# Dropping tokens over capacity: the load of the positions goes behind the first copy of its queue

## The chip, the cores and the metric

The kernel runs on one core of a Trainium2 chip. The metric is the device time of one execution in microseconds (us). The core has compute engines with instruction queues of their own: PE (TensorE, matmuls), DVE (VectorE), ACT (ScalarE), POOL (GpSimd) and SP (SyncE). Transfers are done by 16 DMA engines, which all queues share. In this kernel SP and ACT issue transfers; a transfer that ACT issues stands in ACT's DMA queue (q10 in the profile), one that SP issues in SP's (q1). Each transfer is cut into rows, which are spread over the 16 engines, and each engine adds 1 to a semaphore when its part is done; so a transfer has landed when its semaphore has risen by 16.

## What is computed

```python
def reference(x, token_positions, capacity):       # x: 16 x 1024 x 512 float32
    mask = token_positions < capacity              # token_positions: 16 x 1024, capacity 256
    return (x * mask[..., np.newaxis]).astype(np.float32)
```

Each of the 16,384 tokens has a row of 512 values. A row is kept when the token's position is below the capacity, and set to zero otherwise. The positions of this input are drawn from 0 to 255, so all tokens are kept and the output equals x. The kernel may not assume this; it has to look at the positions.

## The kernel before, in words

The 16,384 rows are seen as 128 groups ("partitions") of 128 tokens (`n_per_p` is 128), so one partition holds 128 x 512 values, 256 KB in a stretch.

The kernel bets on nothing being dropped. It copies x to the output inside the DRAM, without passing through the core's memory: eight transfers of 16 tokens per partition each (L77 to L83, `C = 16`), 4 MB apiece, made of 128 rows of 32 KB. Even transfers are issued by SP, odd ones by ACT, four each. All of them count up the semaphore `s_copy`.

Beside that it finds out whether the bet holds. L72 loads the positions (64-bit integers on the device, so 256 32-bit words per partition, 128 rows of 1 KB) into the tile `tp`; this transfer is issued by ACT and has a semaphore of its own, `s_tp`. DVE waits for it (L102) and works out for every token if it is kept, in four operations over 128x128 elements: `ge`, `lt`, `low`, `keep` (L103 to L117). L119 adds the kept tokens per partition, PE adds the partitions with a matmul against ones (L123), and DVE compares the total with the number of tokens (L125): `drop_i` is 1 if any token is dropped.

SP, ACT and DVE wait for that and read `drop_i` into a register (L130 to L139). If it is 1, they load x piece by piece, multiply each token by its mask and store it over the copy (L140 to L161). If it is 0, as here, they jump over this part. Then ACT and DVE report to SP, SP reports to POOL, which clears the semaphores (L165 to L173), and SP waits for the eight copies (L174), which ends the kernel.

What sets the order around the change: no planner is at work. Each engine's instructions run in the order of the program, and the transfers of one queue stand in it in the order of their issue. The nine early transfers are collected in the list `early` and moved to the head of the program's first block (L86 to L95), ahead of the start-up of the engines, in the order of the list. So ACT's order is: the load, then copies 1, 3, 5, 7; SP's order is: copies 0, 2, 4, 6.

Of the kernel before, what the change touches and what calls it, by code (L numbers as in the profile page):

```python
# [1 line left out]

# [4 lines left out]


@with_exitstack
def kernel(  # L10
    ctx: ExitStack,
    tc: tile.TileContext,
    x: bass.AP,
    token_positions: bass.AP,
    capacity: bass.AP,
    out: bass.AP,
):
    nc = tc.nc
    P = nc.NUM_PARTITIONS
    fp32 = mybir.dt.float32  # L20
    i32 = mybir.dt.int32
    Alu = mybir.AluOpType

    x_f = x.flatten_outer_dims()
    out_f = out.flatten_outer_dims()
    N, D = x_f.shape
    n_per_p = N // P
    cap = float(int(capacity))
    x_r = x_f.rearrange("(p n) d -> p n d", p=P)
    out_r = out_f.rearrange("(p n) d -> p n d", p=P)  # L30
    tp_i32 = token_positions.rearrange("b s -> (b s)").bitcast(i32)

    sp = nc.sync
    act = nc.scalar
    ve = nc.vector
    pe = nc.tensor
    gp = nc.gpsimd


    tc.close()  # L40
    tc.compile()  # L41

    def sbuf(name, shape, dtype):
        return ctx.enter_context(nc.sbuf_tensor(name, shape, dtype)).ap()

    tp = sbuf("tp", [P, 2 * n_per_p], i32)
    ge = sbuf("ge", [P, n_per_p], fp32)
    lt = sbuf("lt", [P, n_per_p], fp32)
    low = sbuf("low", [P, n_per_p], fp32)
    keep = sbuf("keep", [P, n_per_p], fp32)  # L50
    kept = sbuf("kept", [P, 1], fp32)
    ones = sbuf("ones", [P, 1], fp32)
    drop_i = sbuf("drop_i", [1, 1], i32)
    total = ctx.enter_context(nc.psum_tensor("total", [1, 1], fp32)).ap()
    F = 16
    NBUF = 2
    n_fix = n_per_p // F
    xts = [sbuf(f"xt{b}", [P, F, D], fp32) for b in range(NBUF)]

    s_copy = nc.alloc_semaphore("s_copy")  # L60
    s_tp = nc.alloc_semaphore("s_tp")
    s_ve = nc.alloc_semaphore("s_ve")
    s_pe = nc.alloc_semaphore("s_pe")
    s_ld = [nc.alloc_semaphore(f"s_ld{b}") for b in range(NBUF)]
    s_mul = nc.alloc_semaphore("s_mul")
    s_st = [nc.alloc_semaphore(f"s_st{b}") for b in range(NBUF)]
    s_done = nc.alloc_semaphore("s_done")

    n_copy = 0
    early = []  # L70

    load_tp = act.dma_start(out=tp, in_=tp_i32.rearrange("(p w) -> p w", p=P))  # L72
    early.append(load_tp.then_inc(s_tp, 16).ins)

    C = 16  # L77
    for k in range(n_per_p // C):
        ins = (sp, act)[k % 2].dma_start(
            out=out_r[:, k * C : (k + 1) * C, :], in_=x_r[:, k * C : (k + 1) * C, :]  # L80
        ).then_inc(s_copy, 16)
        early.append(ins.ins)
        n_copy += 1  # L83


    home = nc.cur_bb.bb  # L86
    first_bb = nc.cur_f.blocks[0]
    first_sp = next(
        k for k, i in enumerate(first_bb.instructions) if i.engine == mybir.EngineType.SP
    )  # L90
    names = [i.name for i in early]
    home.instructions = [i for i in home.instructions if i.name not in names]
    first_bb.instructions = (
        first_bb.instructions[:first_sp] + early + first_bb.instructions[first_sp:]
    )  # L95

    lo = tp[:, 0 : 2 * n_per_p : 2]
    hi = tp[:, 1 : 2 * n_per_p : 2]


    ve.memset(ones, 1.0).then_inc(s_ve, 1)  # L101
    ve.wait_ge(s_tp, 16)  # L102
    ve.tensor_scalar(  # L103
        out=ge, in0=lo, scalar1=0.0, scalar2=None, op0=Alu.is_ge
    ).then_inc(s_ve, 1)
    ve.wait_ge(s_ve, 2)
    ve.scalar_tensor_tensor(  # L107
        out=lt, in0=lo, scalar=cap, in1=ge, op0=Alu.is_lt, op1=Alu.mult
    ).then_inc(s_ve, 1)
    ve.wait_ge(s_ve, 3)  # L110
    ve.scalar_tensor_tensor(  # L111
        out=low, in0=hi, scalar=0.0, in1=lt, op0=Alu.is_equal, op1=Alu.mult
    ).then_inc(s_ve, 1)
    ve.wait_ge(s_ve, 4)
    ve.scalar_tensor_tensor(  # L115
        out=keep, in0=hi, scalar=0.0, in1=low, op0=Alu.is_lt, op1=Alu.add
    ).then_inc(s_ve, 1)  # L117
    ve.wait_ge(s_ve, 5)
    ve.tensor_reduce(  # L119
        out=kept, in_=keep, axis=mybir.AxisListType.X, op=Alu.add  # L120
    ).then_inc(s_ve, 1)
    pe.wait_ge(s_ve, 6)
    pe.matmul(out=total, lhsT=ones, rhs=kept, start=True, stop=True).then_inc(s_pe, 1)  # L123
    ve.wait_ge(s_pe, 1)
    ve.tensor_scalar(  # L125
        out=drop_i, in0=total, scalar1=float(N) - 0.5, scalar2=None, op0=Alu.is_lt
    ).then_inc(s_ve, 1)


    for e in (sp, act, ve):  # L130
        e.wait_ge(s_ve, 7)
    ET = mybir.EngineType
    drop = nc.values_load(
        drop_i[0:1, 0:1],
        engines=[ET.SP, ET.Activation, ET.DVE],
        min_val=0,
        max_val=1,
        skip_runtime_bounds_check_because="a comparison gives 0 or 1",
    )  # L139
    with nc.If(drop):  # L140
        for u in range(n_fix):
            b = u % NBUF
            if u >= NBUF:
                sp.wait_ge(s_st[b], 16 * (u // NBUF))
            sp.dma_start(out=xts[b], in_=x_r[:, u * F : (u + 1) * F, :]).then_inc(s_ld[b], 16)
            ve.wait_ge(s_ld[b], 16 * (u // NBUF + 1))
            for j in range(F):
                c = u * F + j
                ve.tensor_scalar(
                    out=xts[b][:, j, :],  # L150
                    in0=xts[b][:, j, :],
                    scalar1=keep[:, c : c + 1],
                    scalar2=None,
                    op0=Alu.mult,
                ).then_inc(s_mul, 1)
            if u == 0:
                act.wait_ge(s_copy, 16 * n_copy)
            act.wait_ge(s_mul, (u + 1) * F)
            act.dma_start(out=out_r[:, u * F : (u + 1) * F, :], in_=xts[b]).then_inc(s_st[b], 16)
        for b in range(NBUF):  # L160
            act.wait_ge(s_st[b], 16 * (n_fix // NBUF))  # L161

    for e in (act, ve):  # L165
        e.sem_inc(s_done, 1)
    sp.wait_ge(s_done, 2)
    sp.sem_inc(s_done, 1)
    own = [s_tp, s_ve, s_pe, *s_ld, s_mul, *s_st, s_done]
    ids = sorted(s.num for s in own)  # L170
    assert ids == list(range(ids[0], ids[-1] + 1))
    gp.wait_ge(s_done, 3)
    gp.sem_clear(range(ids[0], ids[-1] + 1))  # L173
    sp.wait_ge(s_copy, 16 * n_copy)  # L174
    sp.sem_inc(s_copy, -16 * n_copy)


# [1 line left out]
_INS = ['x', 'token_positions', 'capacity']  # L179
_OUTS = [((16, 1024, 512), 'float32')]  # L180

_NUMBERS = {'capacity': 256}


# [26 lines left out]
```

## Time and profile before

| | |
|---|---|
| median of 5 runs | 104.58 us (104.35 to 104.81) |
| the profiled execution's own time | 104.48 us |
| its span, first to last instruction | 103.1 us |
| DMA moved in the span | 33.69 MB, mean 327 GB/s |
| HBM read and written together | 652 GB/s over the span |
| busy time of DVE, PE, POOL | 1.5, 0.2, 0.2 us |
| issue to landing of the load of the positions | 2.0 us |
| issue to landing of a copy, SP's and ACT's (median of four) | 61.4 and 67.2 us |

How to read it: the engines' busy times count the arithmetic alone; waiting and issuing transfers are not in them. A row of a DMA queue gives packets, megabytes, and the time that the queue's packets took as a share of what 16 engines have in the span (or in the window asked for). A line of waits names the waiting instruction, what it waited for, the time in total, the number of times, and the longest. "SPq" and "ACTq" are the instruction queues of SP and ACT themselves. A line of the timeline begins with the start and the duration in us.

### The profile page before, as it was taken

What the parts mean: (1) busy time and instruction counts of PE and PEld (TensorE: products, weight loads), DVE (VectorE), ACT (ScalarE), POOL (GpSimd) and SP (SyncE); (2) the same over time, 40 slices, a digit from 0 to 9 for tenths busy, and PEclk for the clock granted to TensorE, in tenths of its full rate; (3) what the DMA queues carried; (4) which work ended last, traced back from release to release, by engine and by line L of the source; (5) the groups of instructions that cost most, each with busy time, mean ns of one, the idle gap of its engine ahead of it and who ended that gap; (6) DMA issues with size and microseconds to landing.
All of it is one profiled execution on the core that took longest, in us unless ns stands there. A gap on an engine that the chain in (4) does not pass through costs nothing. (4 is left out here: it accounts for less than half of the span.)

```text
span 103.1 us, 70 instructions
## 1 busy us (share of the span) xinstructions
PE 0.2 (0%) x2; PEld 0.1 (0%) x2; DVE 1.5 (1%) x7; POOL 0.2 (0%) x4
## 2 busy tenths in 40 slices
PE   0000000000000000000000000000000000000000
PEld 0000000000000000000000000000000000000000
DVE  0230000000000000000000000000000000000000
POOL 0000000000000000000000000000000000000000
DMA  8997989989979999799699797998997998989975
GB/s 254 407 369 241 394 270 356 369 280 356 369 254 407 292 318 407 254 356 381 241 394 381 229 407 254 356 381 280 343 381 254 394 305 305 394 292 330 369 267 178
DMA packets 1297, 33.69 MB, mean 327 GB/s; under 512 B 144, under 2 KB 272, under 8 KB 272
## 3 DMA queue, kind: packets, MB, share of 16 engines
q10 hardware_dynamic: 720, 16.91, 49.7%
q1 hardware_dynamic: 576, 16.78, 48.5%
q14 instruction: 1, 0.01, 0.0%
HBM read 33.69 MB, written 33.55 MB: 652 GB/s over the span
## 5 line engine op out<-in xcount | busy, mean ns | idle before, releaser
L115 DVE SCALAR_TENSOR_TENSOR keep<-tp,low 128x128 f32<-128x128 int32 x1 | 0.3, 293 | 0.0
L107 DVE SCALAR_TENSOR_TENSOR lt<-tp,ge 128x128 f32<-128x128 int32 x1 | 0.3, 291 | 0.0
L111 DVE SCALAR_TENSOR_TENSOR low<-tp,lt 128x128 f32<-128x128 int32 x1 | 0.3, 291 | 0.0
L119 DVE TENSOR_REDUCE kept<-keep 128x1 f32<-128x128 f32 x1 | 0.3, 286 | 0.0
L103 DVE TENSOR_SCALAR ge<-tp 128x128 f32<-128x128 int32 x1 | 0.2, 227 | 0.0
L123 PE MATMUL total<-kept,ones 128*1 128x1 f32 x2 | 0.2, 164 | 6.1 <-DVE kept L119 6.1
L125 DVE TENSOR_SCALAR drop_i<-total 1x1 int32<-1x1 f32 x1 | 0.1, 147 | 0.3 <-PE total L123 0.3
L101 DVE MEMSET ones<- 128x1 f32 x1 | 0.1, 59 | 4.5 <-PEq L41 4.5
L192 POOL MEMSET const-bfloat16-1.0<- 128x1 bf16 x1 | 0.1, 101 | 0.0
L192 POOL MEMSET const-uint8-127<- 128x1 uint8 x1 | 0.1, 101 | 0.0
L192 POOL MEMSET const-float32-1.0<- 128x1 f32 x1 | 0.1, 99 | 0.0
L192 POOL MEMSET const-float32-0.0<- 128x1 f32 x1 | 0.1, 98 | 0.2 <-issue 0.2
L123 PEld LDWEIGHTS total<-kept,ones 128*1 128x1 f32 x2 | 0.1, 82 | 6.1 <-DVE kept L119 6.1
## 6 DMA issues: line engine op xcount, KB each, us to landing
out_dram<-in_x_dram SPq DMA_DIRECT2D x4, 4096.0 KB, 61.4
out_dram<-in_x_dram ACTq DMA_DIRECT2D x4, 4096.0 KB, 67.2
tp<-in_token_positions_dram ACTq DMA_DIRECT2D x1, 128.0 KB, 2.0
```

What stands on the lines that cost most here:

```text
L101: ve.memset(ones, 1.0).then_inc(s_ve, 1)
L103: ve.tensor_scalar(out=ge, in0=lo, scalar1=0.0, scalar2=None, op0=Alu.is_ge).then_inc(s_ve, 1)
L107: ve.scalar_tensor_tensor(out=lt, in0=lo, scalar=cap, in1=ge, op0=Alu.is_lt, op1=Alu.mult).then_inc(s_ve, 1)
L111: ve.scalar_tensor_tensor(out=low, in0=hi, scalar=0.0, in1=lt, op0=Alu.is_equal, op1=Alu.mult).then_inc(s_ve, 1)
L115: ve.scalar_tensor_tensor(out=keep, in0=hi, scalar=0.0, in1=low, op0=Alu.is_lt, op1=Alu.add).then_inc(s_ve, 1)
L119: ve.tensor_reduce(out=kept, in_=keep, axis=mybir.AxisListType.X, op=Alu.add).then_inc(s_ve, 1)
L123: pe.matmul(out=total, lhsT=ones, rhs=kept, start=True, stop=True).then_inc(s_pe, 1)
L125: ve.tensor_scalar(out=drop_i, in0=total, scalar1=float(N) - 0.5, scalar2=None, op0=Alu.is_lt).then_inc(s_ve, 1)
L192: nc = _bacc.Bacc("TRN2", target_bir_lowering=False, num_devices=1)
```

## The change

The load of the positions is issued by ACT after its first copy (copy 1) in place of before it. ACT's order becomes: copy 1, the load, copies 3, 5, 7. SP's order and all else stay as they are.

```diff
-    load_tp = act.dma_start(out=tp, in_=tp_i32.rearrange("(p w) -> p w", p=P))
-    early.append(load_tp.then_inc(s_tp, 16).ins)
-
     C = 16
     for k in range(n_per_p // C):
         ins = (sp, act)[k % 2].dma_start(
             out=out_r[:, k * C : (k + 1) * C, :], in_=x_r[:, k * C : (k + 1) * C, :]
         ).then_inc(s_copy, 16)
         early.append(ins.ins)
         n_copy += 1
+        if k == 1:
+            load_tp = act.dma_start(out=tp, in_=tp_i32.rearrange("(p w) -> p w", p=P))
+            early.append(load_tp.then_inc(s_tp, 16).ins)
```

## The prediction

> **What bounds the kernel now.** I read the page's head and its DMA rows first, then SP's waits, then the timeline of the first microseconds, and last the DMA view cut into short windows.
>
> ```profile
> span 103.1 us, 70 instructions
> DMA  8997989989979999799699797998997998989975
> q10 hardware_dynamic: 720, 16.91, 49.7%
> q1 hardware_dynamic: 576, 16.78, 48.5%
> ...
> SPq L175 <- SPq L175: 95.4, 1, 95.4
> SPq L133 <- DVE drop_i L125: 2.1, 1, 2.1
> ...
> 0.00 2.75 SPq L79 DMA_DIRECT2D out_dram<-in_x_dram  x4
> 0.13 0.39 ACTq L72 DMA_DIRECT2D tp<-in_token_positions_dram  x1
> 0.55 2.59 ACTq L79 DMA_DIRECT2D out_dram<-in_x_dram  x4
> 4.54 0.23 DVE L103 TENSOR_SCALAR ge<-tp 128x128 f32<-128x128 int32 x1
> 6.35 0.15 DVE L125 TENSOR_SCALAR drop_i<-total 1x1 int32<-1x1 f32 x1 [0.28 <-PE total L123]
> ```
>
> The 16 DMA engines are busy from end to end, half for q1 (SP's queue, four copies) and half for q10 (ACT's, four copies and the load: 144 packets more). SP stands at its last wait, for the copies (L175), for 95.4 of 103.1 us, so from 7.7 us on. Everything the load feeds, from ge at 4.54 to SP's arrival at 7.7, is over in 3.2 us and has 95 us to spare. The copies set the end. The load can move the time only through the DMA engines: when their stream begins, how dense it is, and how it ends. For that, the DMA view of 1.0 to 2.2 us, then of 2.2 to 5.7, then of 98.5 to 103.1, with the GB/s of four stretches between:
>
> ```profile
> q1 hardware_dynamic: 16, 0.52, 139.1%
> q10 hardware_dynamic: 144, 0.13, 34.3%
> ...
> q1 hardware_dynamic: 32, 1.05, 80.3%
> ...
> q10 hardware_dynamic: 48, 1.05, 69.2%
> q1 hardware_dynamic: 16, 0.00, 0.2%
> ...
> 1.16:1.52 0.36, 0.00 (x0) 0.00 (x0) 0.00 (x0) 0.00 (x0) 1.00 0.90 287
> 1.52:5.84 4.32, 0.00 (x0) 0.00 (x0) 1.17 (x6) 0.00 (x0) 1.00 1.08 378
> 5.84:99.70 93.86, 0.19 (x2) 0.09 (x2) 0.37 (x2) 0.00 (x0) 1.00 1.01 335
> 99.68:102.78 3.10, 0.00 (x0) 0.00 (x0) 0.00 (x0) 0.00 (x0) 1.00 0.56 180
> ```
>
> (The last two columns of the stretches are the busy share of the DMA engines and GB/s; a packet counts where it starts.) From 1.16 to 1.52 us the engines carry the load alone: 144 packets, 128 of 1 KB and 16 marks of the semaphore, 34.3% of 1.2 us, so 0.41 us on each engine. SP's first 32 KB packets begin at 1.52, as the load's go out. Until 5.84 SP's queue runs alone, three packets on each engine (48 in all); then both queues take turns, one packet each; after 99.68 only ACT's last packets are left, and the last mark falls at 102.78. From 1.16 to 102.78 is 101.6 us of nearly unbroken work.
>
> **The change part by part.** The sum is made against the profiled execution: 104.48 us, its span of 103.1 and 1.4 around it. The median of the five runs is 104.58, so 0.1 is added at the end.
>
> *ACT's issues.* The same five, in another order. Its first copy is issued at 0.13 in place of 0.55 and the load after it, at about 0.13 + 0.58 = 0.71 (ACT's four copies take 2.59 / 4 = 0.65 us each to issue, the shortest 0.58). The later three copies are issued when they are now, since the two durations are only swapped. SP's and POOL's instructions move past nothing. Cost on the path: 0.
>
> *The wait for the load.* On ACT's queue its 144 packets now stand behind the first copy's 144. That copy is issued at 0.55 and, by the DMA view of the microsecond of its issue, lands 30.2 us later, at 30.8. The load then lands at some 32 us if it goes as one turn of its queue, and at about 30.8 + 9 x 1.57 = 45 us if each of its eight rows and its mark on an engine takes a turn against a 32 KB packet of SP's (1.57 us each: 64 on an engine in 101.6 - 0.41 us, with their marks). DVE waits for it at its first real operation; behind that stand its five mask operations and the reduction, PE's matmul, drop_i, then the branch on SP, ACT and DVE, POOL's clearing, and SP's wait for the copies. None of them issues a DMA when nothing is dropped, which is this case: 16.78 MB per queue is all the copying there is. The 3.2 us after landing end at 48 us at the latest. One instruction load of 8 KB is in the trace at 13.8 us, 6 us after the branch; were it to follow the branch, it would come at 54. The cover is the copies until 102.8, so 48 us are left and this costs 0. If the cover were gone, the price would be 3.2 us beyond the load's landing.
>
> *The front of the stream.* Taken out: 0.41 us of small packets ahead of the copies. The question is when SP's first packet can start without them. No row shows it. Lower bound 1.16, where the first packet of any kind starts now; upper bound 1.52, where SP's does now. Nearest row: the load's issue ends at 0.13 + 0.39 = 0.52 and its packets begin 0.64 later; SP's first issue ends at about 0.62 (the median of its four), and 0.62 + 0.64 = 1.26. I take 1.26: the stream begins 0.10 later than now, bounds 0 and +0.36.
>
> *The small packets in the middle.* The same 0.41 us on each engine now lie among large packets. If they cost what they cost now, the length of 101.6 stays as it is: 0. Low bound -0.41: they vanish in the shadow of the other queue's packets, which is not excluded, since a 32 KB packet runs at 32.8 KB / 1.57 us = 20.9 GB/s an engine on the average but SP's alone, in the stretch from 3.22 to 4.45 us, at 453 / 16 = 28: the engines wait on something shared and could catch up. High bound +0.41: each costs double under load. The 112 marks of the copies that fall among large packets show no cost that I can find, which is why I stay at 0.
>
> *The end of the stream.* If the load takes nine turns, SP's queue gains nine packets on ACT's, and ACT's runs alone for about nine more packets at the end, some 14 us in place of the present 3. Is one queue alone slower? Alone at the front: 378 GB/s against 335 with both, so 1.39 us for a round of 16 packets against 1.565: 9 x -0.18 = -1.6 us. Alone at the end: 1.05 MB from about 98.9 to 102.4, 300 GB/s, 1.75 a round: 9 x +0.18 = +1.6. The front has the ramp in it and the end the stragglers, both close to neither; I take 0 and keep half of each, -0.8 and +0.8.
>
> The row on turns is the alternation of single 32 KB packets after 5.84 us. The Trainium skill ("DMA: Bandwidth & Descriptors", Queues, rings and completion order) says that an engine goes round its queues packet by packet, and that a packet is typically some 9 to 17 descriptors. By that, the load's eight rows and mark on an engine could be one turn; the end of the stream would then stay as it is and its term would be 0 for certain, where by the alternation of single descriptors it is the widest term of the sum. Here every 32 KB row is a turn of its own, so for rows of 32 KB this trace does not show such packets; for rows of 1 KB it leaves the question open.
>
> Sum: 0 + 0 + 0.10 + 0 + 0 = +0.1; 104.48 + 0.1 + 0.1 for the median = 104.7 us. Bounds added in full: -1.2 to +1.6.
>
> **The rivals.** A measurement of this kernel (104.35 to 104.81) tells about 0.3%, 0.31 us, from no change; so the marks are 104.27 and 104.89.
> - *Forecast: hidden.* 104.7, own range 104.3 to 104.9. For it: the bytes are the same, and the load has 48 us to spare.
> - *Slower at the front.* SP's first packet is not ready before 1.5 us whatever ACT does; the 0.41 us ahead of it were free, and are now paid among the copies: +0.36, 104.9 to 105.1. For it: SP issues first, at 0.00, and yet its packets come after the load's. Against: they start just as the load's run out, as if held by them. It decides from a start of about 1.4 us on.
> - *Slower at the end.* ACT's queue trails by nine packets and runs alone at the 300 GB/s of the last microseconds: +0.8, 105.5. It decides if a round alone costs 0.035 us more than a shared one (9 x 0.035 = 0.31). For it: the last two rounds. Against: the first three.
> - *Faster.* The small packets vanish among the large ones while the copies begin at 1.26, 0.3 us sooner than now: -0.3; with a lone queue as quick as at the front, -0.8 more is possible: 104.2 to 103.6.
> - *The load decides the end.* It would have to land after 99 us; only one copy of four stands before it. 105 to 107, next to excluded.
>
> **How the numbers follow.** Forecast 0.39. Slower at the front 0.19, at the end 0.18, the load at the end 0.01: together 0.38. Faster 0.23. The range leaves out the far half of "faster" and the far half of "slower at the end": 104.0 to 105.5.
>
> **What the changed profile would show.** ge on DVE starting after 30 us (near 32: one turn; near 45: nine), and SP's last wait shorter by as much: the wait's step right. First DMA packets at 1.26 and of 32 KB: the front right; at 1.5: the first rival. q1's last mark before 90 us with q10 alone behind it: nine turns; then the GB/s of that stretch against 335 decides between the third rival and the fourth. A span of 103.2 with all this is the forecast. It is wrong if the rate with both queues itself changes with the lag between them, which no row of before can show: 1% of it is 1 us.

## The result: 104.74 us, 0.21% over before

The changed kernel takes 104.74 us in the median (104.30 to 105.50, 52 runs), the kernel before, over all its runs beside it, 104.54 us. The ratio is 1.0021, with a 95% interval from 1.0013 to 1.0030: slower by 0.14 to 0.31 us. That lies within the 0.3% that the forecast counts as no change, with a real cost of 0.22 us inside it. A later set of runs on another chip gave 1.0026 (1.0008 to 1.0044). The levels differ from chip to chip (before takes 105.5 to 105.7 us on the chips of the experiments), so below only ratios to before on the same chip are compared, and one profile stands for one execution: the profiled one of the change took 104.95 us, 0.47 us more than the profiled one of before (104.48). That is twice the measured difference, so a cost of 0.2 us is read from the ratios; the traces show only where time could go.

The profile after, in the order of the reading before: the page's DMA rows, SP's and DVE's waits, the timeline.

```profile
span 103.6 us, 70 instructions
q1 hardware_dynamic: 576, 16.78, 48.7%
q10 hardware_dynamic: 720, 16.91, 48.4%
...
SPq L176 <- SPq L176: 58.2, 1, 58.2
SPq L134 <- DVE drop_i L126: 39.4, 1, 39.4
DVE ge L104 <- DMA tp<-in_token_positions_dram: 37.3, 1, 37.3
...
0.12 0.61 ACTq L75 DMA_DIRECT2D out_dram<-in_x_dram  x1
0.77 0.74 ACTq L82 DMA_DIRECT2D tp<-in_token_positions_dram  x1
1.54 1.99 ACTq L75 DMA_DIRECT2D out_dram<-in_x_dram  x3
42.24 0.23 DVE L104 TENSOR_SCALAR ge<-tp 128x128 f32<-128x128 int32 x1 [37.26 <-DMA tp<-in_token_positions_dram]
```

The bytes and packets are the same. The wait for the load is there, 37.3 us of DVE, and ge starts at 42.24 in place of 4.54. SP reaches its last wait 37 us later and still stands there for 58.2 us. So the wait costs nothing. The page's own chain names it nonetheless ("DMA tp", 40% of the span): its last piece is drop_i, before the change as after it, and the copies that set the end are not in it.

What the DMA engines did is seen in the stretches (the last two columns are their busy share and GB/s), and in the DMA view of 29.0 to 40.5 us, where the load is carried:

```profile
1.16:1.38 0.22, 0.00 (x0) 0.00 (x0) 0.00 (x0) 0.00 (x0) 1.00 0.00 0
1.38:4.41 3.03, 0.00 (x0) 0.00 (x0) 0.00 (x0) 0.00 (x0) 1.00 0.99 346
5.84:29.20 23.36, 0.00 (x0) 0.00 (x0) 0.00 (x0) 0.00 (x0) 1.00 1.01 334
42.26:87.88 45.62, 0.19 (x2) 0.09 (x2) 1.52 (x6) 0.00 (x0) 1.00 1.00 333
89.30:101.80 12.50, 0.00 (x0) 0.00 (x0) 0.00 (x0) 0.00 (x0) 1.00 1.00 336
...
q1 hardware_dynamic: 128, 3.67, 94.6%
q10 hardware_dynamic: 128, 0.13, 4.0%
```

The stream begins at 1.38 us; from 1.16, where it began before with the load, to there the engines are idle. In the lower view q1's 128 packets are 7 rounds of copies (a round is one packet on each of the 16 engines) and 16 marks, and q10's 128 are the eight rows of the load on each engine: one turn each, with a packet of SP's between each two, and once SP's mark. The load's packets take 4.0% of 11.5 us, 0.46 us an engine. (In a second trace of the changed kernel, on another chip, they take 3.3% of the 11.0 us from 30.7 to 41.7, 0.36 us.) SP's queue thus gains about eight packets, its last mark falls at 88.54, and from 89.3 to 101.8 ACT's queue runs alone: at 336 GB/s, against 333 with both (328 and 331 in the second trace).

### The profile page after: what moved, and what is told of

Its sections match the earlier page's. It is cut to its first block, busy times and chain, and to the rows that moved or that the text cites. A ratio compares the mean times of both kernels' runs of the same rounds, so it can differ in the third digit from the quotient of the medians.

```text
span 103.6 us, 70 instructions
## 1 busy us (share of the span) xinstructions
PE 0.2 (0%) x2; PEld 0.1 (0%) x2; DVE 1.6 (2%) x7; POOL 0.2 (0%) x4
## 5 line engine op out<-in xcount | busy, mean ns | idle before, releaser
L104 DVE TENSOR_SCALAR ge<-tp 128x128 f32<-128x128 int32 x1 | 0.2, 228 | 37.3 <-DMA tp<-in_token_positions_dram 37.3
```

Source lines behind the costliest of these rows:

```text
L104: ve.tensor_scalar(out=ge, in0=lo, scalar1=0.0, scalar2=None, op0=Alu.is_ge).then_inc(s_ve, 1)
```

## The experiments

Three accounts of the 0.2 us stood against each other. **Front / bytes:** the load's 0.131 MB cost their time at the stream's rate (0.39 us at 333 GB/s) wherever they lie among copies, but ahead of the copies they lie in time in which the engines would be idle for the most part (the first expectations call it "front", the later ones "bytes"). **End:** the queue that trails and runs alone is dearer. **Dear:** small packets among large ones cost more than their bytes.

**No load.** `load_tp` is left out and DVE fills the tile with zeros:

```diff
-    load_tp = act.dma_start(out=tp, ...)
+    ve.memset(tp, 0).then_inc(s_tp, 16)
```

> The load of the positions is left out: DVE fills the tile with zeros and counts as before, so the positions are not looked at. It gives the whole price of the load, ahead of the copies (before) and among them (after). Theory 'front': SP's first packet cannot start before about 1.4 us whether the load stands ahead or not, so of the 0.41 us of small packets ahead only some 0.15 are paid; no_load is 0.1 to 0.2 us (0.1 to 0.2%) under before and 0.3 to 0.45 under after. Theories 'end' (the lone queue and its stragglers cost the 0.2 us) and 'dear' (small packets cost more among large ones): the load ahead is paid in full, no_load is 0.4 us (0.4%) under before.

> No load at all, once more, to narrow its interval (the first gave -0.1% to +0.4%). 'Bytes': 0.07 to 0.12 us (0.1%) under before. 'End' with the load ahead paid in full: 0.4 us (0.4%) under before, which the first run has all but ruled out. If it is over before again, a load ahead of ACT's first copy does something for the stream that its absence does not, and neither theory says what.

Measured 1.0015 (0.9989 to 1.0042) and 0.9992 (0.9974 to 1.0011). By the second, taking the load away gains at most 0.26%, and the two middles lie on either side of no change: a full price of 0.41 us (0.4%) ahead of the copies is ruled out by both. The 0.1% that "bytes" expects lies inside both intervals and is not told from nothing. The reason is in the DMA view of 1.00 to 1.52 us of the first of these kernels:

```profile
DMA  0000000000000000000000000000009990900000
...
q1 hardware_dynamic: 4, 0.13, 92.5%
```

Without a load ahead, SP's first copy packets do not begin before the 31st of 40 slices, at 1.40 us. Before the change they began at 1.52. So the load ahead holds the first copy packets up by 0.12 us in this pair of traces, and the other 0.3 us of it lie in idle time. The 0.12 us is not firm: in two further traces with ACT's load ahead (copy 6 moved and four loads, both below) the first copy packets begin at 1.73 and 1.68 us. But little of such a delay lasts. SP's second round of packets begins at 3.22 to 3.27 us in these three traces, and at 3.16 to 3.30 us in the nine in which no load stands ahead of SP's first copy and SP's queue leads.

**The loose end: a lone queue, without moving the load.** Copy 6 goes from SP to ACT; the load stays ahead.

```diff
-        ins = (sp, act)[k % 2].dma_start(
+        ins = (act if k % 2 or k == 6 else sp).dma_start(
```

> The load stays ahead; copy 6 goes from SP to ACT, so SP has three copies and ACT five, and ACT's queue runs alone for 16 packets more at the end. 'End': 16 / 9 of the change's 0.22 to 0.27 us, 0.4 to 0.5 us (0.4 to 0.5%) over before. 'Bytes': no load among the copies, equal to before within 0.1 us. A lone packet dearer by a third of what 'End' needs (one_queue, with its copies beginning 0.45 us later, leaves 0.4 us over 61 packets): 0.1 us.

Measured 0.9992 (0.9973 to 1.0011). SP's queue has landed its last copy at 75.1 us, and ACT's is alone for the rest. The DMA view of 78.4 to 104 us and two stretches, both queues and ACT's alone:

```profile
q10 hardware_dynamic: 272, 7.86, 92.6%
...
6.50:70.90 64.40, 0.19 (x2) 0.09 (x2) 0.33 (x2) 0.00 (x0) 1.00 0.99 326
80.00:100.00 20.00, 0.00 (x0) 0.00 (x0) 0.00 (x0) 0.00 (x0) 1.00 0.99 329
```

A lone stretch twice as long as the change's costs nothing, where "End" needed 0.4 to 0.5%. "End" is ruled out as the cause. The harder form of it puts all copies in one queue:

```diff
-        ins = (sp, act)[k % 2].dma_start(
+        ins = act.dma_start(
```

> All eight copies are issued by ACT behind the load, none by SP: one queue alone for 64 packets on an engine. 'Bytes': a lone queue runs at the rate of two (336 against 333 GB/s in the trace of after), within 0.5 us of before. 'End': a lone packet costs 0.2 / 9 = 0.02 us more than a shared one, so 61 x 0.02 = 1.4 us (1.3%) over before; at the 300 GB/s that I read from the last microseconds of before, 61 x 0.18 = 11 us over.

Measured 1.0082 (1.0052 to 1.0113), between the two. Part of it is at the front. The DMA view of 1.00 to 1.97 us has the load's packets alone, and the copies begin only after it, at 1.97 in place of 1.52, 0.45 us later:

```profile
q10 hardware_dynamic: 144, 0.13, 45.2%
...
3.00:100.00 97.00, 0.19 (x2) 0.09 (x2) 1.54 (x7) 0.00 (x0) 1.00 1.00 330
```

The other 0.1 to 0.75 us are not explained; the rate alone, 330 GB/s, is no lower than with two queues on the same chip (from 6.5 to 95 us, 326 GB/s with the load behind ACT's last copy and 330 with the load issued by SP, both below).

**The load among the copies, with no long lone stretch of ACT's.** Behind SP's first copy, or from GpSimd in a queue of its own:

```diff
-        if k == 1:
-            load_tp = act.dma_start(out=tp, ...)
+        if k == 0:                                    # behind_sp
+            load_tp = sp.dma_start(out=tp, ...)
```

> The load stands behind SP's first copy in place of ACT's. SP's queue, which leads by two or three packets, gives nine turns and then trails by six or seven, so the lone stretch at the end is SP's and shorter than after the change. 'Bytes': as the change, 0.2 to 0.3 us (0.2 to 0.3%) over before. 'End': about 4 lone packets more than before, 0.1 us over it.

```diff
-    load_tp = act.dma_start(out=tp, ...)              # ahead of the copies
+    gp.dma_start(out=tp, ...).then_inc(s_tp, 16)      # gp_load: after the start-up
```

> The load is issued by GpSimd, in a queue of its own, after the start-up: its packets lie among the first rounds of the copies, and neither SP's nor ACT's queue gives a turn to it. 'Bytes': the load among the copies costs 0.39 us and the front gives 0.1 back, 0.2 to 0.3 us (0.2 to 0.3%) over before, as with the change. 'End': no queue falls behind, no longer lone stretch, equal to before within 0.1 us.

Measured 1.0021 (1.0001 to 1.0040) behind SP's copy and 1.0018 (0.9993 to 1.0042) from GpSimd. The first has the change's ratio, 1.0021, though here SP's queue trails (its last mark falls at 103.86 us; ACT's last copy packet starts at 89.65). The second has the expected middle but an interval that reaches zero. In it the load is cut otherwise, into 32 packets of 4 KB, and lands 15.2 us after its issue while both queues of copies run on:

```profile
q0 software_dynamic: 48, 0.13, 0.5%
tp<-in_token_positions_dram POOLq DMA_DIRECT2D x1, 128.0 KB, 15.2
```

Beside these, the changed kernel once more:

> The changed kernel, unaltered, beside the other three of this set on one chip. Theory 'bytes': the load's 0.131 MB cost their time at the stream's rate, 0.131 MB / 333 GB/s = 0.39 us, when they lie among the copies, and 0.07 to 0.12 us when they lie ahead, where SP's first packet is not ready before 1.40 us anyway: 0.27 to 0.32 us (0.3%) over before. Theory 'end' (the lone queue): the same 0.2 to 0.3, but then one_queue must be several times that.

Measured 1.0026 (1.0008 to 1.0044), as "bytes" has it, and "End" as well: what tells these two apart is the lone queue above.

**More of it.** Four loads into four tiles, ahead of ACT's copies or behind its first one:

```diff
-    load_tp = act.dma_start(out=tp, ...)
-    early.append(load_tp.then_inc(s_tp, 16).ins)
+    for dst in (tp, *more):                           # mid4: the same loop under "if k == 1"
+        load_tp = act.dma_start(out=dst, ...)
+        early.append(load_tp.then_inc(s_tp, 16).ins)
```

> Four loads (into four tiles) ahead of the copies in place of one. All theories: the three more are paid in full, 3 x 0.41 = 1.2 us over before. 'Front' has no other number here, as its free 0.25 us are used up by the first load; this run is the measure for mid4.

> Four loads behind ACT's first copy. ACT's queue gives 36 turns, SP's copies run out in between (near 67 us), and ACT's run alone for about 24 packets in place of 9. 'Front': 3 x 0.46 = 1.4 us over after, 1.6 over before, and so 0.2 to 0.4 over front4. 'Dear' with 0.1 to 0.2 us for each load: 0.5 to 0.9 over front4. 'End': 1.2 over before for the loads and 0.2 x 24 / 9 = 0.5 for the lone stretch, 0.5 over front4, but then split_load must equal before. Small packets in the shadow of the others: below front4.

Measured 1.0091 (1.0070 to 1.0113) ahead and 1.0131 (1.0099 to 1.0163) behind. The run ahead was no such measure as I took it for. Its DMA view of 2.4 to 16 us:

```profile
q1 hardware_dynamic: 149, 4.36, 92.1%
q10 hardware_dynamic: 131, 0.13, 3.1%
```

Only the first load is ahead. The second is carried one row at a time between SP's copy packets, like the change's load, and the two others after it; ACT's first copy starts at 41.9 us. So this kernel has three loads among copies and the other has four, with 0.12 us gained at the front: 0.96 / 3 = 0.32 us each (0.25 to 0.40), and (1.38 + 0.12) / 4 = 0.37 (0.29 to 0.46). Both agree with the 0.39 us of the bytes. For "Dear" little is left here: 0.07 us a load at most.

**Two halves.** The load is cut by partitions, 64 behind each queue's first copy.

```diff
+        if k < 2:
+            h = slice(64 * k, 64 * k + 64)
+            load_tp = (sp, act)[k].dma_start(out=tp[h, :], ...[h, :])
```

> The load is cut in two halves of 64 partitions, one behind SP's first copy and one behind ACT's, so the small packets are still among the copies but neither queue falls behind the other. 'End': the lone stretch is as short as before the change, so the 0.2 us go: equal to before within 0.1 us. 'Front' and 'dear': as after, 0.2 us (0.2%) over before. The load lands near 37 us, since each queue gives five turns in place of nine.

Measured 1.0061 (1.0037 to 1.0084), 0.64 us: "End" missed, and "bytes" too, by a factor of two to three. The DMA view of 26.4 to 29.0 us, where q10's part is its half of the load and the marks of its first copy:

```profile
q1 hardware_dynamic: 95, 0.56, 76.3%
q10 hardware_dynamic: 80, 0.07, 25.2%
```

25.2% of 2.6 us is 0.66 us an engine for half a load, where the whole load took 0.46 and 0.36 in the two traces of the change, among large packets of the other queue. In this one execution the small packets of two queues, taking turns with each other, had records about three times as long or more. That fits the extra cost, and would be "Dear" for small packets that meet small packets; that it is the cause was not tested by itself.

**The load by SP at the front.** The one attempt at a version better than both:

```diff
-    load_tp = act.dma_start(out=tp, ...)
+    load_tp = sp.dma_start(out=tp, ...)
```

> The load is issued by SP ahead of its first copy, ACT begins with its first copy. SP issues first, at 0.00, so the load's packets can begin at about 1.03 and be done at 1.45, when ACT's first copy packets come (in after they were ready by then at the earliest). 'Bytes': the load is free altogether, 0.1 us (0.1%) under before, hardly to be told from it. If the load's place at the front has no free time: equal to before.

Measured 1.0052 (1.0031 to 1.0072): a miss, 0.55 us slower and not the 0.1 us faster that "bytes" gave. The load's packets did begin earlier, at 1.02 us, and ACT's first copy at 1.51. Two things are different: the load is on SP's queue, and ACT's queue of copies now leads while SP's trails. Which of them costs half a microsecond, and why, stays open; the profiled execution, 105.68 us, is the fastest of the ten and no slower than before (105.72), so its trace cannot show it. "Bytes" has no account of this run.

**No cover.** The load goes behind ACT's last copy (`if k == 7`).

> The load is issued behind ACT's last copy, so no copy is left to cover it. Both theories: the masks and the branch come after the last copy's landing. The load lands about 0.4 us after the last copy's packets, then 3.2 us until SP is at its last wait: 3 to 4 us over before, 107.5 to 108.5 on a chip that gives before 104.5. If the time stays within 1 us of before, the cover was not what hid the wait.

Measured 1.0407 (1.0372 to 1.0443), 4.3 us. Its timeline and SP's wait:

```profile
105.07 0.23 DVE L104 TENSOR_SCALAR ge<-tp 128x128 f32<-128x128 int32 x1 [100.33 <-DMA tp<-in_token_positions_dram]
106.88 0.14 DVE L126 TENSOR_SCALAR drop_i<-total 1x1 int32<-1x1 f32 x1 [0.28 <-PE total L124]
SPq L134 <- DVE drop_i L126: 102.5, 1, 102.5
```

From ge at 105.07 to the end of the span at 108.4 there are 3.3 us, as priced, and nobody waits for copies any more. Of the other 1.0 us, some 0.5 lie outside the span: a run takes 1.8 us more than its span here, and 1.3 to 1.4 us more in the runs of before beside it. The load's own last packets and landing share the remainder. So the cover of the copies is what hides the wait.

## Why the prediction was right, point by point

- *What bounds the kernel:* right. The copies' stream sets the end in every version that keeps the load ahead of the last copy.
- *ACT's issues:* its later copies were to be issued when they are now. They came 0.4 us later (1.54 in place of 1.13), since the load's issue took 0.74 us and not 0.39 behind a copy. With a queue of work in front it cost nothing.
- *The wait:* right, and near the later of its two cases. Nine turns of 1.57 us behind a landing at 30.8 were to give 45. ge started at 42.24: the marks of ACT's first copy fell 1.6 us sooner (median 28.2 in place of 29.8), since it was issued sooner and waited for two packets of SP's at the start in place of three, and one of the turns went to SP's mark, which takes no time. The 8 KB instruction load that I let follow the branch did follow it, from 13.8 to 50.1 us, and had 50 us to spare.
- *The front:* the mechanism was right and the size was off. I took SP's first packet to be ready at 1.26 us, by the time from the end of an issue to its first packet; it was at 1.38 (1.40 without any load). The stream begins 0.22 us later than before, not 0.10, well within the bounds of 0 and 0.36. This is the term that was mis-sized.
- *The small packets in the middle:* 0.46 us in place of 0.41 in the profile, 0.36 in the second trace of the same kernel: +0.05 or -0.05 against 0 taken; not hidden, not doubled.
- *The end:* 0 was right, and the reason could have been kept narrower: 336 GB/s alone against 333, and 329 against 326 with copy 6 moved. The widest bounds of the sum, 0.8 us either way, came from the ramp at the front and the stragglers at the end, which are no rates of a lone queue.
- *The sum:* 0.22 + 0.05 = 0.27 by the terms of the one profile, 0.17 with the second trace's load, against +0.1 forecast and 0.22 (0.14 to 0.31) measured. So the forecast was right in that next to nothing happens, and about half of the measured cost; that the terms of single traces come so near the ratio is in part luck, since these two executions lie 0.47 us apart.
- *The rivals:* "slower at the front" named the cause that fits best, free time ahead of SP's first packet, and claimed more of it (+0.36) than there was; "slower at the end" fell with the rate of the lone queue, and "faster" with the measured time and the unhidden small packets.
- *The lag between the queues*, the prediction's last sign of being wrong, was not tested by itself. The load gives SP's queue a lead of some ten packets over ACT's in place of two. In the profile the rate is 334 GB/s ahead of the load and 333 behind it, so a change of 1%, 1 us, did not come; one of 0.2% would be all of the measured cost, and such a stretch cannot tell it. Against it stand the load behind SP's copy, with another lag and the same ratio, and the load from GpSimd, with the old lag, whose interval reaches zero. So "bytes" is the account that fits most of the runs, not one shown alone: the two halves and the load by SP went against it.
- *Two small slips:* behind the load stand four mask operations and the reduction, not five and the reduction; and 64 packets in 101.6 - 0.41 us are 1.58 us each, not 1.57. Neither moves the sum.

On turns the trace decides against what I weighed from the Trainium skill ("DMA: Bandwidth & Descriptors", Queues, rings and completion order), by which an engine drains a packet of typically some 9 to 17 descriptors before it goes on to the next queue. Here the 1 KB rows went singly, a 32 KB packet of SP's between each two.

## What to carry to other kernels

A stream of transfers that fills the DMA engines from the first microsecond to the last can leave free time ahead of its first packets. Here a load of 128 KB that ACT issued into it cost too little to measure, and the same load among the copies cost about its bytes at the stream's rate. That is no rule for every such place: issued by SP ahead of the copies, or cut in two halves among them, it cost 0.55 and 0.64 us, which is not explained. Whether a load's landing is late matters only against the cover left at its place, so read that from the last wait of the engine that ends the kernel. A load behind a copy does not land behind that copy: each of its rows waits a turn against the other queue's large packets, here 13 us for 128 KB.

## What the runs showed of the hardware that was not expected

- Two DMAs issued ahead in one queue are not both ahead: the first load of four had its packets alone from 1.18 us, the second gave a turn to SP's queue for every row, and ACT's first copy began at 41.9 us.
- One queue moves DRAM-to-DRAM copies of 32 KB rows at the rate of two: 336 and 333 GB/s in the changed kernel, 328 and 331 in its second trace, 329 and 326 with copy 6 moved.
- Which queue carries the load ahead of the copies is not neutral: with it on SP's queue, and so ACT's copies leading, the same transfers took 1.0052 (1.0031 to 1.0072) of the time that they take with it on ACT's. No run here explains it.
